# Half of a decoder's retention projection as a seven-product group, with three buffers and the first loads moved

## The chip, the cores and the metric

The kernel runs on one core of one Trainium2 chip. The metric is device time in microseconds (us), the median of several runs. A core has a matrix engine (TensorE, PE in the profile, with its weight loads as PEld), three engines for elementwise work (VectorE: DVE, ScalarE: ACT, GpSimd: POOL) and a synchronisation engine (SP) that here issues only the weight loads. All five run their own instruction streams in order and meet at semaphores. Data lies in the on-chip SBUF, matmul results in eight PSUM banks of 128 x 512 fp32.

## The reference

Two layers, each with a retention branch and an mLSTM branch that read one combined projection of x, merge gates, an output product, and a SwiGLU block; D_MODEL 1024, SEQ 512, DEPTH 2, four heads with q/k of 128 and v of 256 in each branch.

```python
for l in range(DEPTH):
    proj = x @ w_in[l]
    (r_q, r_k, r_v, r_g, m_qk, m_v, m_o, m_i, m_f, g_a, g_b) = jnp.split(proj, IN_OFFSETS, axis=-1)
    ...
    o_ret = _head_norm(_retention(rq, rk, rv), ret_norm_g[l]) * jax.nn.silu(r_g.astype(f32))
    y_ret = o_ret.astype(dt) @ w_proj_ret[l]
    ...
    y_ml = o_ml.astype(dt) @ w_proj_mlstm[l]
    gate_a = jax.nn.sigmoid(g_a + b_merge[l, :D_MODEL])
    gate_b = jax.nn.sigmoid(g_b + b_merge[l, D_MODEL:])
    mix = (gate_a * y_ret + gate_b * y_ml) @ w_out[l]
    x = _layer_norm(DEEPNORM_ALPHA * x + mix, ln1_g[l], ln1_b[l])
    gu = x @ w_gate_up[l]
    hidden = jax.nn.silu(gu[..., :D_FF]) * gu[..., D_FF:]
    x = _layer_norm(DEEPNORM_ALPHA * x + hidden @ w_down[l], ln2_g[l], ln2_b[l])
```

The change touches `y_ret` (1024 x 1024 weights times 1024 x 512 activations), and the places where other values are kept.

## The kernel before, in words

**Products in three parts.** Every fp32 number is split into a high part, rounded to the matrix engine's fp32r type, and the low rest. A product is three matmuls: high by high, high by low, low by high. The high part of a weight unit is a copy on ACT (`hi_to`, L201), the low part a subtraction on DVE (`lo_of`, L133).

**Units and groups.** Weights come in units of 128 x 1024 fp32 (512 KB), loaded by SP in a fixed order into a ring of five raw buffers; high and low parts have rings of five too, and preparation runs four units ahead. `feat` (L272) multiplies one unit with the whole activation: 24 matmuls of 512 columns into one main bank, then an evacuation. `quad` (L304) takes four units at once, as a 2 x 2 block product of the Strassen-Winograd kind: seven products p1, p3, p5, p7, p6, p2, p4, each of 24 matmuls of 256 columns, in place of eight. Its operands are four plain weight blocks and three or four sums of blocks (T1, T2, T3 on DVE in `sum_to`, L187 to L191; T4 on POOL, L223), and on the activations' side four sums of quarters, which `input_sums` makes for one block of 128 rows at a time: two additions of high and low part on POOL (`xs`, L589), four sums on DVE (`sf`, L595), a high copy on ACT and a low subtraction on DVE. Product p3 reads the fourth sum.

**Order.** PE's and SP's instructions run as the program writes them. ACT, DVE and POOL get an order from a scheduler, except inside most groups, where the written order holds. Work that PE doesn't do at once lies in a queue of generators (`side`); `slot()` runs one step of it after every few matmuls, and `drain()` what is left. The heads' attention work, the transposes, `input_sums` and `fetch` (L560 to L565: reads a branch's result back from HBM and splits it) are such generators.

**Banks.** Four PSUM banks are "main" (`pm`) and four auxiliary (`pa`). The value columns of a branch and then its gate columns are computed token by token (`tok_units`, L360 to L362) in four main banks each; head work takes auxiliary banks.

**The stage that changes.** After the merge gates, whose last groups read x, the retention result (`orh`, `orl`) is multiplied with its projection: eight `feat` calls with `ya_evac` (L912), each an evacuation on DVE that multiplies with the gate `sga`. Beside them `fetch` brings in the mLSTM result (`om`, in the big pair that is not x's), whose eight `feat` calls follow; then the mixing product reads `mx`, which lies where x was. One pool of four scratch buffers (tag `sc`) serves `xs`, `sf`, `of`, the groups' evacuations and the first x loads.

**The start.** x is loaded in six pieces, four of 128 x 512 on ACT's queue and two of 128 x 1024 on SP's, between the slices of the first four weight units (L424); ACT copies the high parts (L433), and `first_units` (L343 to L345) multiplies as the pieces land.

Of the kernel before, what the change touches and what calls it, by code (L numbers as in the profile page):

```python
# [53 lines left out]
def layer_plan():  # L54
# [34 lines left out]
    for j in range(2, FT, 2):  # L89
        for c in (0, DFF):  # L90
# [8 lines left out]
QUADS = [layer_plan().index(("F", w, c + j * P)) for w, c, js in (("in", O_MQK, (0, 2)), ("in", O_GA, (0, 4)),  # L99
                                                                  ("in", O_GB, (0, 4)), ("gu", 0, range(2, FT, 2))) for j in js]  # L100
UNIT_IF = layer_plan().index(("F", "if", 0))
# [3 lines left out]
def decoder_trunk(ctx: ExitStack, tc: tile.TileContext, wall, xT_in, x_in, pvec, lnp, rtab, out):  # L105
# [311 lines left out]
    for i in range(NFIRST):  # L417
        firsts.append([wp.tile([P, UNIT], F32, tag="raw", name="wraw", bufs=NRAW),
                       wp.tile([P, UNIT], F32R, tag="hi", name="whi"), wp.tile([P, UNIT], F32R, tag="lo", name="wlo")])
    k0 = 0  # L420
    for n in (1, 1, 1, 1, 2, 2):
        t = scratch([P, n, S], "xraw")
        ks, cs = slice(k0, k0 + n), slice(k0 * P, (k0 + n) * P)
        (nc.scalar if n == 1 else nc.sync).dma_start(t, xT_in[:, ks, :])  # L424
        for i, (r, hi, lo) in enumerate(firsts):
            nc.sync.dma_start(r[:, cs], wall[i][:, cs])
        if k0 == 0:
            nc.vector.tensor_copy(xh[:, ks, :], t)
        else:
            nc.scalar.copy(xh[:, ks, :], t)  # L430
        lo_of(xl[:, ks, :], t, xh[:, ks, :])
        for r, hi, lo in firsts:
            nc.scalar.copy(hi[:, cs], r[:, cs])  # L433
            lo_of(lo[:, cs], r[:, cs], hi[:, cs])
        k0 += n
    for i, (r, hi, lo) in enumerate(firsts):
# [22 lines left out]
    def scores(qk, hh, box, mult, key_weight, query_weight):  # L459
# [5 lines left out]
        for c in range(2):  # L465
            pa = aux_bank()
            t0, t1, t2 = c * HC, c * HC + P, (c + 1) * HC
            nc.tensor.matmul(pa[:, :HC], lhsT=k[:, t0:t1], rhs=q[:, t0:t2], start=True, stop=True)  # L468
            nc.tensor.matmul(pa[:, HC:W1], lhsT=k[:, t1:t2], rhs=q[:, t1:t2], start=True, stop=True)
            pf = scratch([P, W1], "pf")  # L470
            mult(pf, pa, c)
            hi, lo = pp[:, 2 * c * W1 : (2 * c + 1) * W1], pp[:, (2 * c + 1) * W1 : (2 * c + 2) * W1]
            nc.scalar.copy(hi, pf)
            lo_of(lo, pf, hi)
            yield
        pa = aux_bank()
        for j in range(2):
# [20 lines left out]
    def weighted(box, vh, vl, hh, nv, done):  # L498
# [3 lines left out]
        val = lambda j: (vh[:, j, hh, :], vl[:, j, hh, :])  # L502
        pa = aux_bank()
        for j in range(2):
# [5 lines left out]
        for i in range(NB):  # L510
            c, e = i // 2, i % 2
            pa = aux_bank()
            w = [(0, e * P)] + ([(1, HC)] if e else [])
            for n, (j, o) in enumerate(w):
                three(pa[:, :nv], cut(2 * c * W1 + o, P, W1), val(2 * c + j), n == 0, c == 0 and n == e)
            if c:
                three(pa[:, :nv], cut(O_QD + e * P, P, HC), st, False, True)
            done(i, pa)
            yield

    def head_norms(oo, p, gt, gain, od):
# [22 lines left out]
        for hh in range(2):  # L544
            m = 2 * (2 * p + hh)
            t = scratch([P, 2, S], "ot")
            for f in range(2):
                pa = aux_bank()
                for b in range(NB):
# [21 lines left out]
    class Halves:  # L571
# [32 lines left out]
    for l in range(L):  # L604
# [62 lines left out]
        def if_cols():  # L667
            r3 = rows[:, 3]
            pa = aux_bank()
            for b in range(NB):  # L670
# [5 lines left out]
        for p in range(2):  # L676
# [42 lines left out]

            tok_units([main_bank() for _ in range(NB)], lambda k: xh[:, k], lambda k: xl[:, k], K8, True, True, v_evac)  # L720
            oo = reg.tile([P, 2, NB, DV], F32, tag="oo", name="roo")
# [14 lines left out]

            tok_units([main_bank() for _ in range(NB)], lambda k: xh[:, k], lambda k: xl[:, k], K8, True, True, g_evac)
            drain()
            gain = pv[:, C_RG : C_RG + 8]
            side.append(head_norms(oo, p, gt, gain, od[0]))  # L740
# [42 lines left out]
        for p in range(2):  # L783
# [142 lines left out]
        mxh, mxl = bigpair(cur, f"mx{l}")

# [306 lines left out]
```

## Time and profile before

| what | value |
|---|---|
| median of three runs | 1776.27 us (1775.71 to 1776.57) |
| the profiled execution | 1776.88 us |
| its span | 1775.2 us |
| mean granted clock of PE | 0.998 |
| PE busy | 1760.3 us, 99% |
| DVE, ACT, POOL busy | 1311.3, 793.9, 432.9 us |

The page and the trace come from the profiled execution. A line of the timeline gives start and duration of an instruction in us, engine, program line, operation, output and inputs by their names, the shape, and in brackets how long the engine had been idle and what ended that. The start-to-start distance of neighbours is their cost, since durations overlap a little. A line of the waits gives who waited, for whom, total us, how often, and the longest. A line of the windows gives a stretch, the busy time of PE, PEld, DVE, ACT and POOL, the granted clock (1.00 is full) and the share and rate of the DMA engines.

### The profile page before, as it was taken

Reading aid. Unit: us, or ns where it says so; the run is one execution under the profiler, and the core shown is the slowest. Engines: PE = TensorE matmul, PEld = TensorE weight load, DVE = VectorE, ACT = ScalarE, POOL = GpSimd, SP = SyncE. Lnnn points to the kernel's source line nnn. Section 1 sums busy time; section 2 is a strip of 40 time slices with the busy share of each in tenths; the row PEclk is TensorE's granted clock in tenths of the full one; section 3 lists DMA queues with packets and bytes.
Section 4 is the critical chain, followed back from the end, with each engine's and each line's share of the span. In section 5 each row is a group of like instructions: output and inputs, shape, how many; then the busy total and the mean of one; then the engine's idle time right before and its main releaser. Section 6 shows DMA issues by size and latency. Waiting matters only on the chain.

```text
span 1775.2 us, 27167 instructions
## 1 busy us (share of the span) xinstructions
PE 1760.3 (99%) x10904; PEld 1586.0 (89%) x10904; DVE 1311.3 (74%) x1735; ACT 793.9 (45%) x1157; POOL 432.9 (24%) x321
## 2 busy tenths in 40 slices
PE   9999999999999999999999999999999999999997
PEld 7888898998889999988898898989988899999886
DVE  7686878795559999863476868787845699998534
ACT  5445555663226444451244455556533254445310
POOL 2141110231001555520121311112300115555200
PEclk9999999999999999999999999999999999999999
DMA  7222422346333333363243323313553223333521
GB/s 253 91 91 81 142 79 88 111 141 235 96 114 109 99 96 108 107 213 96 84 166 91 110 86 107 119 60 108 201 179 119 96 95 107 111 116 112 187 70 48
DMA packets 76174, 209.49 MB, mean 118 GB/s; under 512 B 6760, under 2 KB 9832, under 8 KB 75024
## 3 DMA queue, kind: packets, MB, share of 16 engines
q1 hardware_dynamic: 65632, 167.27, 29.5%
q0 software_dynamic: 9840, 39.43, 6.3%
q8 instruction: 86, 1.41, 0.3%
q10 hardware_dynamic: 576, 1.05, 0.2%
q14 instruction: 40, 0.33, 0.1%
HBM read 190.93 MB, written 16.79 MB: 117 GB/s over the span
## 4 chain that ended last, share of the span: by engine, by line
PE 97%; DVE 1%; DMA 1%; ACT 1%; issue 0%; SPq 0%; DVEq 0%
PE pm L324 31%; PE pm L360 9%; PE pm L362 9%; PE pm L361 9%; PE pm L267 5%; PE pm L266 5%; PE pm L268 5%; PE pa L324 5%; PE pa L361 3%; PE pa L360 3%; PE pa L362 3%; PE pa L494 1%; PE pa L495 1%; PE pa L496 1%; PE pa L550 1%; PE pa L468 1%
## 5 line engine op out<-in xcount | busy, mean ns | idle before, releaser
L133 DVE TENSOR_TENSOR wlo<-wraw,whi 128x1024 fp32r<-128x1024 f32 (+2 forms) x424 | 597.0, 1421 | 201.9 <-ACT whi L201 198.9
L201 ACT CAST whi<-wraw 128x1024 fp32r<-128x1024 f32 x402 | 419.9, 1049 | 471.0 <-PE pm L267 115.2
L450 POOL TENSOR_TENSOR rs<-ve,nhalf 128x4 f32<-128x4 f32 (+1 forms) x32 | 31.9, 997 | 482.6 <-DVE ve L449 482.6
L223 POOL TENSOR_TENSOR wraw<-wraw 128x1024 f32<-128x1024 f32 x32 | 77.0, 2406 | 151.2 <-issue 57.9
L360 PE MATMUL pm<-whi,x0h 128*128 128x512 f32 x256 | 102.9, 402 | 1.5 <-DVE rvl L133 1.5
L360 PE MATMUL pm<-whi,x20h 128*128 128x512 f32 x256 | 102.5, 400 | 0.6 <-DVE rvl L133 0.6
L362 PE MATMUL pm<-wlo,x0h 128*128 128x512 f32 x256 | 100.7, 393 | 0.0
L361 PE MATMUL pm<-whi,x0l 128*128 128x512 f32 x256 | 100.4, 392 | 0.0
L362 PE MATMUL pm<-wlo,x20h 128*128 128x512 f32 x256 | 100.3, 392 | 0.0
L361 PE MATMUL pm<-whi,x20l 128*128 128x512 f32 x256 | 100.1, 391 | 0.0
L1085 POOL TENSOR_TENSOR qa<-qa 128x512 f32<-128x512 f32 x20 | 42.8, 2141 | 142.6 <-DVE qa L1084 90.6
L324 PE MATMUL pm<-x10h,whi 128*128 128x256 f32 x240 | 67.9, 283 | 0.0
L324 PE MATMUL pm<-x10l,whi 128*128 128x256 f32 x240 | 67.9, 283 | 0.0
L324 PE MATMUL pm<-s0h,whi 128*128 128x256 f32 x240 | 67.9, 283 | 0.0
L324 PE MATMUL pm<-s0l,whi 128*128 128x256 f32 x240 | 67.9, 283 | 0.0
L324 PE MATMUL pm<-s0h,wlo 128*128 128x256 f32 x240 | 67.9, 283 | 0.0
L324 PE MATMUL pm<-x11h,whi 128*128 128x256 f32 x240 | 67.9, 283 | 0.0
L324 PE MATMUL pm<-x11l,whi 128*128 128x256 f32 x240 | 67.9, 283 | 0.0
L324 PE MATMUL pm<-x11h,wlo 128*128 128x256 f32 x240 | 67.9, 283 | 0.0
L324 PE MATMUL pm<-s1h,whi 128*128 128x256 f32 x240 | 67.9, 283 | 0.0
L324 PE MATMUL pm<-s1l,whi 128*128 128x256 f32 x240 | 67.9, 283 | 0.0
L324 PE MATMUL pm<-s1h,wlo 128*128 128x256 f32 x240 | 67.9, 283 | 0.0
(519 smaller groups left out, 5675.2 us busy)
## 6 DMA issues: line engine op xcount, KB each, us to landing
wraw<-wall SPq DMA_DIRECT2D x306, 512.0 KB, 3.8
od<-ot POOLq DMA_DIRECT2D x16, 512.0 KB, 3.6
of<-od POOLq DMA_DIRECT2D x16, 512.0 KB, 5.0
gb<-lnp POOLq DMA_DIRECT2D x4, 1024.0 KB, 6.2
x1d<-xr POOLq DMA_DIRECT2D x8, 512.0 KB, 2.9
xr<-x1d POOLq DMA_DIRECT2D x8, 512.0 KB, 4.8
negm<-md POOLq DMA_DIRECT2D x2, 1026.0 KB, 6.6
xr<-xtok POOLq DMA_DIRECT2D x4, 512.0 KB, 6.8
```

Source lines behind the costliest of these rows:

```text
L133: nc.vector.tensor_tensor(out=out_lo, in0=full, in1=hi.bitcast(F32), op=ALU.subtract)
L201: nc.scalar.copy(hi, sum_t[i])
L223: nc.gpsimd.tensor_tensor(out=raw_t[u + 2], in0=raw_t[u], in1=raw_t[u + 3], op=ALU.add)
L266: nc.tensor.matmul(pm[:, c0:c1], lhsT=hi[:, k], rhs=xh[:, k, c0:c1], start=(k == 0), stop=False)
L267: nc.tensor.matmul(pm[:, c0:c1], lhsT=hi[:, k], rhs=xl[:, k, c0:c1], start=False, stop=False)
L268: nc.tensor.matmul(pm[:, c0:c1], lhsT=lo[:, k], rhs=xh[:, k, c0:c1], start=False, stop=(k == KT - 1))
L324: nc.tensor.matmul(pm, lhsT=x[:, j, k], rhs=y[:, k], start=go and n == 0, stop=j == 1 and k == 3 and n == 2, skip_group_check=not first)
L360: nc.tensor.matmul(pm, lhsT=sh(k)[:, a], rhs=hi[:, j], start=first, stop=False)
L361: nc.tensor.matmul(pm, lhsT=sl(k)[:, a], rhs=hi[:, j], start=False, stop=False)
L362: nc.tensor.matmul(pm, lhsT=sh(k)[:, a], rhs=lo[:, j], start=False, stop=last)
L450: nc.gpsimd.tensor_tensor(out=rs[:, :n], in0=ve[:, :n], in1=nhalf[:, :n], op=ALU.pow)
L1085: nc.gpsimd.tensor_tensor(out=v, in0=v, in1=u, op=ALU.subtract)
```

## The change

1. The last four of the eight units of the retention projection become one seven-product group, with a new evacuation `ya_ev`: ACT copies p1 and p5, DVE takes the others, and POOL two subtractions and six multiplications with half of a gate each. It needs `input_sums` of the retention result and the sums T1 to T4 of those weights. `in_turn` interleaves these input sums with the `fetch` of the mLSTM result during the first four `feat` calls.
2. Three homes rotate: `om` takes the place of x, the new sums `rs` the place of the earlier sums, and the mixing input four tiles that held values (`vh`, `vl`), gates (`gt`) and head outputs (`oo`).
3. The gate stream (second token stream of a pair of heads) takes the four auxiliary banks, and head work during it main ones (`stream_banks`, `head_bank`).
4. All six x loads are issued on ACT's queue before anything else there; the last two go to a tile of their own, `x_late`.

Below are rows of the engines' orders, before and after. DVE around the retention stage, before: `om0l` is the low part of a fetched mLSTM piece, `sga` the evacuation of a unit.

```order
L889 TENSOR_TENSOR ga<-pm,ga 128x512
L133 TENSOR_TENSOR wlo<-wraw,whi 128x1024
L133 TENSOR_TENSOR om0l<-of,om0h 128x1024
L912 TENSOR_TENSOR sga<-pm,sga 128x512
L133 TENSOR_TENSOR om0l<-of,om0h 128x1024
L133 TENSOR_TENSOR wlo<-wraw,whi 128x1024
L912 TENSOR_TENSOR sga<-pm,sga 128x512
L133 TENSOR_TENSOR wlo<-wraw,whi 128x1024
L912 TENSOR_TENSOR sga<-pm,sga 128x512
```

And after, the last piece of the sums, up to the fourth and last `rs0l` (`sf` are the sums, the `wraw` row is T2):

```order
L608 TENSOR_TENSOR sf<-sf,xs 128x256
L144 TENSOR_TENSOR om0l<-of,om0h 128x1024
L144 TENSOR_TENSOR wlo<-wraw,whi 128x1024
L144 TENSOR_TENSOR rs0l<-sf,rs0h 128x4x256
L927 TENSOR_TENSOR sga<-pm,sga 128x512
L608 TENSOR_TENSOR sf<-xs 128x256 x2
L608 TENSOR_TENSOR sf<-sf,xs 128x256
L144 TENSOR_TENSOR wlo<-wraw,whi 128x1024
L608 TENSOR_TENSOR sf<-sf,xs 128x256
L202 TENSOR_TENSOR wraw<-wraw 128x1024
L927 TENSOR_TENSOR sga<-pm,sga 128x512
L144 TENSOR_TENSOR rs0l<-sf,rs0h 128x4x256
```

Between two evacuations stood one or two operations of 1024 columns; now there are four to seven rows, the sums among them.

POOL in the same place, after (before, it held only the fetches `of` and the loads `xr` there): the additions `xs`, two by two or four, and the weight sum T4 (`wraw`).

```order
L898 TENSOR_TENSOR ga<-ga 128x512
L899 TENSOR_TENSOR gc<-gc,ga 128x512
L602 TENSOR_TENSOR xs<-orh,orl 128x512 x2
L571 DMA of<-od 128x1024
L602 TENSOR_TENSOR xs<-orh,orl 128x512 x4
L571 DMA of<-od 128x1024
L234 TENSOR_TENSOR wraw<-wraw 128x1024
L571 DMA of<-od 128x1024
```

All additions but the first two now stand behind the last evacuation of the merge gates (`ga`, `gc`).

ACT at the start, before, with the semaphores that a row waits for:

```order
L424 DMA xraw<-xt 128x512 x3
L433 ACT_TABLE_LOAD
L433 CAST whi<-wraw 128x128 [waits DMAHW1_49]
L433 CAST whi<-wraw 128x128 [waits DMAHW2_49]
L433 CAST whi<-wraw 128x128 [waits DMAHW4_49]
L433 CAST whi<-wraw 128x128 [waits DMAHW5_49]
L430 CAST x0h<-xraw 128x512 [waits DMAHW3_49]
L433 CAST whi<-wraw 128x128 [waits DMAHW7_49]
```

And after:

```order
L434 DMA xraw<-xt 128x512 x3
L434 DMA xraw<-xt 128x512 [waits DMAHW0_49]
L434 DMA x_late<-xt 128x1024 [waits DMAHW3_49]
L434 DMA x_late<-xt 128x1024 [waits DMAHW7_49]
L445 ACT_TABLE_LOAD
L445 CAST whi<-wraw 128x128 [waits DMAHW1_49]
L445 CAST whi<-wraw 128x128 [waits DMAHW2_49]
```

The three later loads now stand ahead of the table load and of the first cast. By the casts' waits, semaphore 0 is that of the first x piece, 3 of the second, and 7 of the fifth weight slice.

The core of the diff:

```diff
-                                                                  ("in", O_GB, (0, 4)), ("gu", 0, range(2, FT, 2))) for j in js]
+                                                                  ("in", O_GB, (0, 4)), ("ret", 0, (4,)), ("gu", 0, range(2, FT, 2))) for j in js]
...
+    def head_bank():
+        return main_bank() if turned["now"] else aux_bank()
+
+    def stream_banks(second):
+        turned["now"] = second
+        return [aux_bank() if second else main_bank() for _ in range(NB)]
...
-    k0 = 0
-    for n in (1, 1, 1, 1, 2, 2):
-        t = scratch([P, n, S], "xraw")
+    x_late = reg.tile([P, 4, S], F32, tag="gt", name="x_late")
+    x_raw = [(k, 1, scratch([P, 1, S], "xraw")) for k in range(4)] + [(k, 2, x_late[:, k - 4 : k - 2]) for k in (4, 6)]
+    for k0, n, t in x_raw:
+        nc.scalar.dma_start(t, xT_in[:, k0 : k0 + n, :])
+    for k0, n, t in x_raw:
         ks, cs = slice(k0, k0 + n), slice(k0 * P, (k0 + n) * P)
-        (nc.scalar if n == 1 else nc.sync).dma_start(t, xT_in[:, ks, :])
...
-            pa = aux_bank()
+            pa = head_bank()
...
-            tok_units([main_bank() for _ in range(NB)], lambda k: xh[:, k], lambda k: xl[:, k], K8, True, True, g_evac)
+            tok_units(stream_banks(True), lambda k: xh[:, k], lambda k: xl[:, k], K8, True, True, g_evac)
             drain()
+            turned["now"] = False
...
-        omh, oml = bigpair(oth, f"om{l}")
-        side.append(fetch(od[1], [omh[:, :4], omh[:, 4:]], [oml[:, :4], oml[:, 4:]]))
-        for m in range(8):
+        def ya_ev(m):
+            t = {}
+
+            def times(src, i, half, eng):
+                for j in range(2):
+                    g = sga[m + 2 * i + j][:, half * HC : (half + 1) * HC]
+                    eng.tensor_tensor(out=g, in0=src[:, j * HC : (j + 1) * HC], in1=g, op=ALU.mult)
+
+            def ev(name, banks):
+                two = lambda n: t.setdefault(n, scratch([P, 2, S], n))
+                if name == "p1":
+                    nc.scalar.copy(two("ra")[:, 0], banks["a"])
+                elif name == "p5":
+                    nc.scalar.copy(two("ra")[:, 1], banks["c"])
+                elif name == "p7":
+                    nc.vector.tensor_tensor(out=two("rc")[:, 1], in0=t["ra"][:, 1], in1=banks["d"], op=ALU.subtract)
+                elif name == "p6":
+                    u, v = t["ra"][:, 0], t["ra"][:, 1]
+                    nc.vector.tensor_tensor(out=u, in0=banks["b"], in1=u, op=ALU.add)
+                    nc.gpsimd.tensor_tensor(out=v, in0=v, in1=u, op=ALU.subtract)
+                    nc.gpsimd.tensor_tensor(out=t["rc"][:, 1], in0=t["rc"][:, 1], in1=u, op=ALU.subtract)
+                elif name == "p2":
+                    times(banks["a"], 0, 0, nc.vector)
+                    nc.vector.tensor_tensor(out=t["rc"][:, 0], in0=banks["e"], in1=t["ra"][:, 1], op=ALU.add)
+                elif name == "p4":
+                    nc.vector.tensor_tensor(out=t["ra"][:, 1], in0=banks["d"], in1=t["ra"][:, 0], op=ALU.add)
+
+                    def rest():
+                        times(t["rc"][:, 0], 1, 0, nc.gpsimd)
+                        times(t["rc"][:, 1], 1, 1, nc.gpsimd)
+                        times(t["ra"][:, 1], 0, 1, nc.gpsimd)
+                    return rest
+            return ev
+
+
+        omh, oml = bigpair(cur, f"om{l}")
+        rsh, rsl = sum_views(oth, f"rs{l}")
+        pending = [input_sums(Halves(orh), Halves(orl), rsh, rsl), fetch(od[1], [omh[:, :4], omh[:, 4:]], [oml[:, :4], oml[:, 4:]])]
+
+        def in_turn():
+
+            n = 0
+            while pending:
+                n += 1
+                for g in pending[:1] * (n % 2) + pending[-1:] if len(pending) > 1 else list(pending):
+                    if next(g, "end") == "end":
+                        pending.remove(g)
+                yield
+
+        side.append(in_turn())
+        for m in range(4):
             feat(Halves(orh), Halves(orl), ya_evac(m))
+        with tc.manual_schedule(engines=ordered):
+            quad(Halves(orh), Halves(orl), rsh, rsl, ya_ev(4))
         drain()
...
-        mxh, mxl = bigpair(cur, f"mx{l}")
+        mxs = [reg.tile([P, 4, S], F32R, tag=t, name=f"mx_{t}") for t in ("vh", "vl", "gt", "oo")]
+        mxh, mxl = Halves(mxs[:2]), Halves(mxs[2:])
```

More of the change, by code (lines that the diff above doesn't have):

```diff
@@ L122, in aux_bank @@
         return psa.tile([P, 512], F32, tag="a", name="pa")
+    turned = {"now": False}
+    def head_bank():
[3 more added lines that the diff above has]
+        return [aux_bank() if second else main_bank() for _ in range(NB)]
     def scratch(shape, name):
@@ L434, in decoder_trunk @@
             lo_of(lo[:, cs], r[:, cs], hi[:, cs])
-        k0 += n
     for i, (r, hi, lo) in enumerate(firsts):
@@ L475, in scores @@
             yield
-        pa = aux_bank()
+        pa = head_bank()
         for j in range(2):
@@ L502, in weighted @@
         val = lambda j: (vh[:, j, hh, :], vl[:, j, hh, :])
-        pa = aux_bank()
+        pa = head_bank()
         for j in range(2):
@@ L511, in weighted @@
             c, e = i // 2, i % 2
-            pa = aux_bank()
+            pa = head_bank()
             w = [(0, e * P)] + ([(1, HC)] if e else [])
@@ L547, in head_norms @@
             for f in range(2):
-                pa = aux_bank()
+                pa = head_bank()
                 for b in range(NB):
@@ L577, in __getitem__ @@
         def __getitem__(self, a):
+            if isinstance(a[1], slice):
+                return self.ts[a[1].start // 4][:, :, a[2]]
             return self.ts[a[1] // 4][:, a[1] % 4, a[2]] if len(a) == 3 else self.ts[a[1] // 4][:, a[1] % 4]
@@ L668, in if_cols @@
             r3 = rows[:, 3]
-            pa = aux_bank()
+            pa = head_bank()
             for b in range(NB):
@@ L718, in v_evac @@
                 lo_of(vl[:, b], src, vh[:, b])
-            tok_units([main_bank() for _ in range(NB)], lambda k: xh[:, k], lambda k: xl[:, k], K8, True, True, v_evac)
+            tok_units(stream_banks(False), lambda k: xh[:, k], lambda k: xl[:, k], K8, True, True, v_evac)
             oo = reg.tile([P, 2, NB, DV], F32, tag="oo", name="roo")
@@ L827, in v_evac @@
                 lo_of(vl[:, b, :, :DV], src, vh[:, b, :, :DV])
-            tok_units([main_bank() for _ in range(NB)], lambda k: xh[:, k], lambda k: xl[:, k], K8, True, True, v_evac)
+            tok_units(stream_banks(False), lambda k: xh[:, k], lambda k: xl[:, k], K8, True, True, v_evac)
             oo = reg.tile([P, 2, NB, DV], F32, tag="oo", name="moo")
@@ L850, in g_evac @@
                 nc.scalar.activation(gt[:, b], pm, AF.Sigmoid)
-            tok_units([main_bank() for _ in range(NB)], lambda k: xh[:, k], lambda k: xl[:, k], K8, True, True, g_evac)
+            tok_units(stream_banks(True), lambda k: xh[:, k], lambda k: xl[:, k], K8, True, True, g_evac)
             drain()
+            turned["now"] = False
             gain = pv[:, C_MG : C_MG + 8]
```

## The prediction, made before the result was known

> **What bounds the kernel now.** I read the page first, then the chain of waits, then PE's own waits, and last the timeline of the stage that is changed.
>
> ```profile
> span 1775.2 us, 27167 instructions
> PE 1760.3 (99%) x10904; PEld 1586.0 (89%) x10904; DVE 1311.3 (74%) x1735; ACT 793.9 (45%) x1157; POOL 432.9 (24%) x321
> PE 97%; DVE 1%; DMA 1%; ACT 1%; issue 0%; SPq 0%; DVEq 0%
> PE pm L360 <- DVE rvl L133: 2.0, 2, 1.5
> PE pm L344 <- DVE wlo L133: 1.6, 2, 0.8
> ```
>
> PE is busy for 99% of the span and is 97% of the chain; its waits are a few us in all. So the end moves by what is taken from PE's matmuls and by any wait that is newly put in front of them. DVE's 74% is a mean; what counts is DVE's load in the 22 us in which the new sums have to be made.
>
> The sum below is made against the profiled execution (1776.88 us, of which the span is 1775.2), 0.6 above the median of 1776.27. A measurement of this kernel can tell about 0.2%, 3.6 us, from no change.
>
> **1. Fewer matmuls in the retention projection.** Eight units run today from the first `orh` matmul to the first `om0h` one:
>
> ```profile
> 404.93 0.40 PE L266 MATMUL pm<-orh,whi 128*128 128x512 f32 x1
> 449.46 0.40 PE L266 MATMUL pm<-om0h,whi 128*128 128x512 f32 x1
> 359.01 17.28 PE pm L324 x144
> 376.29 2.88 PE pa L324 x24
> ```
>
> That is 44.53 us for 192 matmuls, or 0.232 each; four units take 22.27. The chain of waits shows a group of seven products without a gap: 144 matmuls in 17.28 and 24 in 2.88, so 168 in 20.16. Saved: 2.11 per layer, **-4.2** in two layers. If no wait arose, this would be all of it.
>
> **2. The sums of the retention activations, made on DVE and POOL.** The second product (p3) takes the fourth sum, in four blocks of 128 rows. Its first three blocks occupy 9 matmuls of 0.12 us, so PE needs the last block's lo part at 404.93 + 22.27 + 2.88 + 1.08 = 431.2. Is it there? DVE works in its own order. From the end of the evacuation at 404.09 (L887 before, L902 now) to the fourth `rs0l`, the change puts in DVE's queue: 14 operations of 1024 columns (5 `wlo`, 3 weight sums T1 to T3, 2 `om0l`, 4 `rs0l`), 5 evacuations of 512 with a PSUM source, and 16 `sf` of 256. Prices, start to start:
>
> ```profile
> 101.81 0.41 DVE L595 TENSOR_TENSOR sf<-sf,xs 128x256 f32<-128x256 f32 x1
> 102.14 1.21 DVE L133 TENSOR_TENSOR wlo<-wraw,whi 128x1024 fp32r<-128x1024 f32 x1
> 103.28 0.41 DVE L595 TENSOR_TENSOR sf<-sf,xs 128x256 f32<-128x256 f32 x1
> 404.09 0.69 DVE L887 TENSOR_TENSOR gc<-pm,ga 128x512 f32<-128x512 f32 x1 [1.19 <-POOL ga L883]
> 404.70 1.69 DVE L133 TENSOR_TENSOR om0l<-of,om0h 128x1024 fp32r<-128x1024 f32 x1
> 404.50:448.60 44.10, 44.10 (x194) 35.83 (x194) 21.58 (x22) 15.22 (x20) 4.03 (x7) 1.00 0.58 198
> ```
>
> 0.33 for a `sf` (101.81 to 102.14), 1.14 for 1024 columns (102.14 to 103.28), 0.61 for a PSUM evacuation (404.09 to 404.70). So 16.0 + 3.0 + 5.3 = 24.3 us of DVE work from 404.7 on: it ends at 429.0, 2.2 us ahead of PE, if DVE is never held. The windows view (PE, PEld, DVE, ACT, POOL, the clock) says that today DVE is busy 21.58 of the whole 44.1 us there; the change wants more than that in the first half.
>
> DVE is held, by POOL. The change puts 8 additions `xs` of 512 columns (two of them while DVE still works for the group before) and the weight sum T4 on POOL:
>
> ```profile
> 401.86 2.20 POOL L883 TENSOR_TENSOR ga<-ga 128x512 f32<-128x512 f32 x1 [1.00 <-DVE ga L882]
> 404.02 1.29 POOL L884 TENSOR_TENSOR gc<-gc,ga 128x512 f32<-128x512 f32 x1
> 616.89 1.22 DVE L133 TENSOR_TENSOR wlo<-wraw,whi 128x1024 fp32r<-128x1024 f32 x1
> 625.98 7.57 DVE L133 TENSOR_TENSOR wlo<-wraw,whi 128x1024 fp32r<-128x1024 f32 x3
> 625.59 2.41 POOL L223 TENSOR_TENSOR wraw<-wraw 128x1024 f32<-128x1024 f32 x1 [2.35 <-issue]
> 627.96 4.52 POOL L1067 TENSOR_TENSOR hf_vl<-qb,qc 128x512 f32<-128x512 f32 x2
> ```
>
> Three `wlo` that should take 3 x 1.14 = 3.4 took 7.57 beside 2.41 + 4.52 us of POOL, while POOL's own additions stretched from 1.29 (at 404.02, beside an evacuation that took its usual 0.69) to 2.26 each. Two operations that both read SBUF run in turn, not together; one with a PSUM source isn't touched. So I add POOL's time to DVE's: 8 x 1.29 + 2.4 = 12.7, less at most 3.0 that falls beside the five evacuations: 9.7 to 12.7. DVE ends at 438.7 to 441.7, PE waits 7.5 to 10.5. Bounds: 0 (no sharing cost) and 10.5. I take **9.0 per layer, +18.0**, nearest to the row of 7.57. A wait can't be under nothing. What is queued behind on DVE (the weights' lo parts of later products, 1.14 each against 2.88 per product) catches up. The four casts on ACT and the three more hi copies lie beside this: ACT is busy 15.22 of 44.1 there. The six half-width multiplications of the new evacuation are on POOL behind the group's last product, and nobody waits for them before the mixing stage.
>
> The Trainium skill ("GPSIMD Engine Reference", section 1, Specifications) says that GpSimd's SBUF interfaces are shared with VectorE, with contention against instructions that have two SBUF inputs. The trace agrees, with 7.57 for 3.4 and an untouched 0.69 with a PSUM input. By that rule the sum stays as it is.
>
> **3. The clock after a wait.** One stall today shows what a pause costs beyond itself:
>
> ```profile
> 59.68 0.50 PE L360 MATMUL pm<-whi,x0h 128*128 128x512 f32 x1 [1.47 <-DVE rvl L133]
> 60.26:63.67 3.41, 3.41 (x13) 2.93 (x12) 2.51 (x4) 0.42 (x2) 0.00 (x0) 0.50 0.57 163
> 63.67:67.08 3.41, 3.41 (x20) 2.93 (x19) 1.03 (x3) 0.54 (x2) 0.00 (x0) 1.00 0.32 129
> 940.54 0.50 PE L360 MATMUL pm<-whi,x20h 128*128 128x512 f32 x1 [0.57 <-DVE rvl L133]
> ```
>
> After 1.47 us of idleness PE ran 3.41 us at a granted clock of 0.50, which loses half of it, 1.7. A wait of 9 us should bring that at least once: **+1.7 per layer, +3.4**, bounds 0 and 6.8 (two windows each).
>
> The Trainium skill ("TensorE: Matmul & The Clock Gate", Part 1) puts the drop behind at least one idle window of about 3.4 us. Here it followed on 1.47 us, so the measurement decides. By the page, waits of 9 us drop the clock too.
>
> **4. The second stream's banks.** The gate stream no longer waits for the values' evacuation: it starts in the auxiliary banks, and the head work takes main ones. The 1.47 of layer 0, its 1.7 of half clock and the 0.57 of layer 1 are on offer, 3.7. But six matmuls later (1.4 us) the first head product stands in a main bank and reads `rvl` blocks that come from DVE in the same row of evacuations, 0.6 apart; I leave 0.8 in. **-2.9**, bounds 0 and -3.7.
>
> **5. The start.** All six x loads stand at the head of ACT's queue. The fourth to sixth wait, by the order, for the first x, the second x and the fifth weight slice to land, and the table load and the first cast are queued behind:
>
> ```profile
> 0.81 1.37 ACTq L424 DMA_DIRECT2D xraw<-xt  x3
> ...
> 2.21 1.28 ACT L433 ACT_TABLE_LOAD   x1 [2.21 <-issue]
> 4.17 0.30 ACT L433 CAST whi<-wraw 128x128 fp32r<-128x128 f32 x1 [0.69 <-DMA wraw<-wall]
> 5.00 0.77 PE L343 MATMUL pm<-x0h,whi 128*128 128x512 f32 x1
> 6.61 0.67 ACT L433 CAST whi<-wraw 128x128 fp32r<-128x128 f32 x2 [1.31 <-DMA wraw<-wall]
> 7.71 0.69 ACT L433 CAST whi<-wraw 128x128 fp32r<-128x128 f32 x3
> 18.55 0.50 PE L344 MATMUL pm<-x0h,wlo 128*128 128x512 f32 x1 [0.80 <-DVE wlo L133]
> 30.71 0.39 PE L285 MATMUL pm<-x0h,whi 128*128 128x512 f32 x1
> ```
>
> The third slice had landed at 6.61 and the fifth (first of the three at 7.71) by 7.71; I take 7.2. Add one DMA issue (1.37 / 3 = 0.5), the table load 1.28 and the 0.83 from first cast to first matmul (4.17 to 5.00): PE begins at 9.8 instead of 5.00, +4.8 (4.2 to 5.3). Against it: the first four units ran from 5.00 to 30.71, 25.7 us for 96 matmuls that at 0.232 take 22.3. Up to 3.4 us of waits, such as that at 18.55, go if x is early and the later start lets the weights get ahead. And PE, whose warming matmuls end before the first cast is there, may begin at half clock (+1.7, as in part 3). Bounds +1.4 (4.8 - 3.4) and +6.5 (4.8 + 1.7); I take **+2.5**.
>
> **6. Homes.** The rotated buffers add no operation. `om` now goes where x was, and x is read until 404.93, so its copies begin some 4 us later; PE wants them after the retention stage, 20 us and more behind that. `rs` takes the place of the earlier sums, and the mixing input that of values, gates and head outputs, done by then. Priced at 0, hidden by the four feats and the group; without that cover it is one wait of about an `om0l`, 1.7.
>
> Sum: -4.2 + 18.0 + 3.4 - 2.9 + 2.5 = +16.8, so 1776.9 + 16.8 = **1793.7**.
>
> **Rivals.**
> *A, DVE gets there (faster).* Place: p3's fourth block; price: no wait. It decides if POOL's 12.7 cost DVE less than 2.2 us. For it: DVE alone ends at 429.0, and two `xs` come early. Against it: the 7.57 row. -4.2 - 2.9 + 2.5 = -4.6: 1772.3.
> *B, a partial wait.* POOL's additions fall into DVE's gaps; 4 us per layer and no clock drop: -4.2 + 8 - 2.9 + 2.5 = +3.4: 1780.3. Against it: DVE's queue has hardly a gap before 429.
> *C, full waits, clock kept.* +16.8 - 3.4: 1790.3. For it: the 0.57 at 940.54 left the clock alone. Against: 1.47 did not.
> *D, worse.* POOL and DVE pass four scratch buffers to and fro (`xs`, `sf`, the fetched `of` and the evacuation's own), so each also waits for the other: 12 per layer, the start at +6.5 and nothing from the banks: -4.2 + 24 + 3.4 + 6.5 = +29.7: 1806.6.
> That the change doesn't do what it says I leave out: PE's order holds 144 rows more, 2 x (168 - 96).
>
> **How the numbers follow.** Forecast 0.55, A 0.15, B 0.10, C 0.12, D 0.08. The forecast's own range, with PE's waits of 7.5 to 10.5 and the bounds of the start, is 1786 to 1802. For 8 in 10 I leave out A and half of D: 1776 to 1805. Faster by over 0.2% means below 1772.7: most of A, 0.13. Within 0.2%: the rest of A and most of B, 0.09. Slower: 0.78.
>
> **What would show it.** Right: PE waits in the second product of both retention groups for `rs0l` from DVE, 7 to 11 us each, with a clock of 0.50 behind them; three lo operations or sums stretched beside `xs`; the first matmul at 9 to 10; no wait of the gate stream for `rvl`. Wrong: a retention group that runs in 20.2 us without a wait (A), or a wait that ends on ACT or a DMA instead of DVE.

## The result and the profile after

The changed kernel takes 1794.07 us (median of four runs, 1793.69 to 1794.6) against 1776.25 for the kernel before: a ratio of 1.0103, 95% interval 1.0090 to 1.0115. It is slower by 17.8 us, and its profiled span is 1792.4 us against 1775.2, 17.2 more.

The head of the page:

```profile
span 1792.4 us, 27563 instructions
PE 1761.0 (98%) x11048; PEld 1596.0 (89%) x11048; DVE 1365.2 (76%) x1791; ACT 810.4 (45%) x1175; POOL 494.9 (28%) x355
```

PE's waits (who waited, for whom, total us, how often, longest):

```profile
PE pm L335 <- DVE rs0l L144: 4.4, 2, 3.1
PE pm L354 <- ACT whi L445: 4.3, 1, 4.3
PE pm L335 <- DVE rs1l L144: 4.2, 2, 3.0
PE pm L335 <- ACT rs0h L609: 3.7, 1, 3.7
PE pm L335 <- ACT rs1h L609: 3.6, 1, 3.6
```

PE's busy time has hardly moved although it has fewer columns to stream, which already says that part of it runs more slowly. The wait for `rvl` is gone from the list. New are 8.0 us (layer 0: 4.4 + 3.7) and 7.8 us (layer 1) at L335, the group's matmuls, and 4.3 at the first matmul. PE's timeline at those places, layer 0:

```profile
9.13 0.80 PE L354 MATMUL pm<-x0h,whi 128*128 128x512 f32 x1 [4.34 <-ACT whi L445]
...
404.80 0.40 PE L277 MATMUL pm<-orh,whi 128*128 128x512 f32 x1
...
427.01 0.28 PE L335 MATMUL pm<-orh,whi 128*128 128x256 f32 x1
...
432.19 0.38 PE L335 MATMUL pm<-rs0l,whi 128*128 128x256 f32 x1 [1.31 <-DVE rs0l L144]
...
436.35 0.58 PE L335 MATMUL pm<-rs0h,whi 128*128 128x256 f32 x1 [3.65 <-ACT rs0h L609]
439.98 0.58 PE L335 MATMUL pm<-rs0l,whi 128*128 128x256 f32 x1 [3.05 <-DVE rs0l L144]
...
458.23 0.39 PE L277 MATMUL pm<-om0h,whi 128*128 128x512 f32 x1
```

The retention stage lasts from 404.80 to 458.23, 53.43 us, where it was 44.53. By the rates of before its matmuls need 22.27 + 20.16 = 42.43; 8.0 are the three waits, inside p3: for the low part of the third block of the sums, and for the high and then the low part of the fourth; 3.0 are left. The windows view shows most of what those are (columns as before; the clock is the third number from the end):

```profile
435.00:438.00 3.00, 0.58 (x1) 0.29 (x1) 3.00 (x4) 2.60 (x5) 1.50 (x1) 0.50 0.26 25
438.00:441.00 3.00, 1.02 (x5) 1.02 (x6) 3.00 (x3) 0.94 (x1) 1.35 (x2) 0.50 0.65 217
441.00:444.00 3.00, 3.00 (x16) 3.00 (x16) 2.33 (x3) 0.79 (x1) 0.53 (x1) 0.50 0.66 184
444.00:447.00 3.00, 3.00 (x23) 3.00 (x23) 2.36 (x2) 1.24 (x3) 0.06 (x1) 0.86 1.01 388
```

The clock is at 0.50 from 435 until after 444. And this is why the sums were late, on DVE and POOL:

```profile
410.27 2.29 DVE L198 TENSOR_TENSOR wraw<-wraw 128x1024 f32<-128x1024 f32 x1
...
419.94 1.22 DVE L144 TENSOR_TENSOR wlo<-wraw,whi 128x1024 fp32r<-128x1024 f32 x1
...
421.42 0.68 DVE L927 TENSOR_TENSOR sga<-pm,sga 128x512 f32<-128x512 f32 x1
423.95 0.76 DVE L608 TENSOR_TENSOR sf<-xs 128x256 f32<-128x256 f32 x2 [1.85 <-POOL xs L602]
...
426.43 2.33 DVE L144 TENSOR_TENSOR om0l<-of,om0h 128x1024 fp32r<-128x1024 f32 x1
428.68 2.32 DVE L144 TENSOR_TENSOR wlo<-wraw,whi 128x1024 fp32r<-128x1024 f32 x1
430.93 1.21 DVE L144 TENSOR_TENSOR rs0l<-sf,rs0h 128x1024 fp32r<-128x1024 f32 x1
...
436.87 3.05 DVE L144 TENSOR_TENSOR rs0l<-sf,rs0h 128x1024 fp32r<-128x1024 f32 x1
```

POOL's timeline of the same stretch:

```profile
410.18 3.54 POOL L602 TENSOR_TENSOR xs<-orh,orl 128x512 f32<-128x512 f32 x2 [2.76 <-ACT sgb L884]
...
419.11 4.80 POOL L602 TENSOR_TENSOR xs<-orh,orl 128x512 f32<-128x512 f32 x2 [0.36 <-DVE rs0l L144]
426.26 3.66 POOL L602 TENSOR_TENSOR xs<-orh,orl 128x512 f32<-128x512 f32 x2 [2.35 <-DVE rs0l L144]
...
436.50 2.34 POOL L234 TENSOR_TENSOR wraw<-wraw 128x1024 f32<-128x1024 f32 x1 [6.08 <-ACT rs0h L609]
```

Beside the `xs` at 410 and 426 and beside T4, DVE's operations of 1024 columns take 2.29 to 3.05 instead of 1.2. Beside the `xs` at 419 it is the other way round: DVE's `wlo` at 419.94 takes its usual 1.22, the two `xs` take 4.80, and DVE is then idle for 1.85 us until they are done. From 406.80 to the end of the last `rs0l` at 439.92 that is DVE's only pause. And the last two pairs of `xs` wait for an `rs0l` on DVE, which frees their scratch buffer: so the two engines hold each other up in that way too. The cast on ACT for which PE waits 3.65 us is itself late because of DVE: it starts as soon as DVE's last `sf` is done.

```profile
435.25 1.04 ACT L609 CAST rs0h<-sf 128x1024 fp32r<-128x1024 f32 x1 [0.23 <-DVE sf L608]
```

Where the time went, stage by stage, from the starts of PE's matmuls in the two traces:

| stage | before | after | difference |
|---|---|---|---|
| to the end of the first units | 30.71 | 33.66 | +2.95 |
| from there to the sums of the first mLSTM group (173.06, 172.94) | 142.35 | 139.28 | -3.07 |
| retention stage, layer 0 | 44.53 | 53.43 | +8.90 |
| mixing product, layer 0 | 45.32 | 45.78 | +0.46 |
| its end to the next layer's first matmul | 349.34 | 348.98 | -0.36 |
| layer 1, to the sums of its first mLSTM group | 164.71 | 164.06 | -0.65 |
| retention stage, layer 1 | 44.53 | 53.24 | +8.71 |
| mixing product, layer 1 | 45.32 | 45.77 | +0.45 |
| all others | | | -0.2 |

### The profile page after: what moved, and what is told of

Read it like the earlier page. It is cut to its first block, busy times and chain, and to the rows that moved or that the text cites. A ratio compares the mean times of both kernels' runs of the same rounds, so it can differ in the third digit from the quotient of the medians.

```text
span 1792.4 us, 27563 instructions
## 1 busy us (share of the span) xinstructions
PE 1761.0 (98%) x11048; PEld 1596.0 (89%) x11048; DVE 1365.2 (76%) x1791; ACT 810.4 (45%) x1175; POOL 494.9 (28%) x355
## 5 line engine op out<-in xcount | busy, mean ns | idle before, releaser
L144 DVE TENSOR_TENSOR wlo<-wraw,whi 128x1024 fp32r<-128x1024 f32 (+2 forms) x430 | 613.2, 1440 | 211.2 <-ACT whi L212 205.8
L212 ACT CAST whi<-wraw 128x1024 fp32r<-128x1024 f32 x408 | 426.7, 1049 | 453.2 <-PE pa L372 104.6
L234 POOL TENSOR_TENSOR wraw<-wraw 128x1024 f32<-128x1024 f32 x34 | 81.6, 2400 | 163.7 <-issue 57.9
L335 PE MATMUL pm<-x10h,whi 128*128 128x256 f32 x240 | 67.9, 283 | 0.0
L335 PE MATMUL pm<-x10l,whi 128*128 128x256 f32 x240 | 67.9, 283 | 0.0
L335 PE MATMUL pm<-s0h,whi 128*128 128x256 f32 x240 | 67.9, 283 | 0.0
L335 PE MATMUL pm<-s0l,whi 128*128 128x256 f32 x240 | 67.9, 283 | 0.0
L335 PE MATMUL pm<-s0h,wlo 128*128 128x256 f32 x240 | 67.9, 283 | 0.0
L335 PE MATMUL pm<-x11h,whi 128*128 128x256 f32 x240 | 67.9, 283 | 0.0
L335 PE MATMUL pm<-x11l,whi 128*128 128x256 f32 x240 | 67.9, 283 | 0.0
L335 PE MATMUL pm<-s1h,whi 128*128 128x256 f32 x240 | 67.9, 283 | 0.0
L335 PE MATMUL pm<-s1l,whi 128*128 128x256 f32 x240 | 67.9, 283 | 0.0
L335 PE MATMUL pm<-s1h,wlo 128*128 128x256 f32 x240 | 67.9, 283 | 0.0
L335 PE MATMUL pm<-x10h,wlo 128*128 128x256 f32 x240 | 67.9, 283 | 0.0
L335 PE MATMUL pm<-x11h,wlo 128*128 128x256 f32 x240 | 67.9, 283 | 0.0
L202 DVE TENSOR_TENSOR wraw<-wraw 128x1024 f32<-128x1024 f32 x34 | 52.3, 1538 | 0.0
L371 PE MATMUL pa<-whi,x0h 128*128 128x512 f32 x128 | 51.4, 402 | 0.0
L371 PE MATMUL pa<-whi,x20h 128*128 128x512 f32 x128 | 51.4, 402 | 0.0
L634 POOL TENSOR_TENSOR rqk<-rqk,rt 128x512 f32<-128x512 f32 x16 | 33.3, 2082 | 65.1 <-DVE rt L633 65.1
L371 PE MATMUL pm<-whi,x0h 128*128 128x512 f32 x128 | 51.1, 399 | 0.0
```

Source lines behind the costliest of these rows:

```text
L144: nc.vector.tensor_tensor(out=out_lo, in0=full, in1=hi.bitcast(F32), op=ALU.subtract)
L202: nc.vector.tensor_tensor(out=f, in0=f, in1=e, op=ALU.add)
L212: nc.scalar.copy(hi, sum_t[i])
L234: nc.gpsimd.tensor_tensor(out=raw_t[u + 2], in0=raw_t[u], in1=raw_t[u + 3], op=ALU.add)
L335: nc.tensor.matmul(pm, lhsT=x[:, j, k], rhs=y[:, k], start=go and n == 0, stop=j == 1 and k == 3 and n == 2, skip_group_check=not first)
L371: nc.tensor.matmul(pm, lhsT=sh(k)[:, a], rhs=hi[:, j], start=first, stop=False)
```

## The experiments

Times are medians, each beside the median of the kernel before on the same chip.

| kernel | us | before | difference |
|---|---|---|---|
| the change | 1794.07 | 1776.25 | +17.8 |
| x loads put back | 1793.56 | 1775.35 | +18.2 |
| group taken out | 1776.12 | 1775.35 | +0.8 |
| `xs` on DVE | 1787.14 | 1775.35 | +11.8 |
| `xs` as a copy on ACT | 1772.90 | 1775.35 | -2.5 |
| banks alone | 1772.99 | 1776.33 | -3.3 |
| start alone | 1776.42 | 1776.33 | +0.1 |
| idle matmuls in p3 | 1792.06 | 1776.33 | +15.7 |
| group in the mLSTM projection | 1772.52 | 1776.33 | -3.8 |
| x loads put back, `x_late` kept | 1791.88 | 1776.02 | +15.9 |
| mLSTM group, `x_late` kept | 1770.14 | 1776.02 | -5.9 |
| mLSTM group, start as changed | 1773.40 | 1776.07 | -2.7 |
| mLSTM group, late x on POOL's queue | 1770.42 | 1776.07 | -5.7 |

**Is it the group?** The change with eight plain units:

```diff
-("ret", 0, (4,)), ("gu", ...
+("gu", ...
...
-        for m in range(4):
+        for m in range(8):
             feat(Halves(orh), Halves(orl), ya_evac(m))
-        with tc.manual_schedule(engines=ordered):
-            quad(Halves(orh), Halves(orl), rsh, rsl, ya_ev(4))
```

> The change without the seven-product group: eight plain units in the retention projection, no input sums; homes, banks and start as changed. Theory (the whole loss is the group's waits on DVE and the clock behind them): 1776.3 - 3.7 (banks) + 3.0 (start) = 1775.5 us, 1774.5 to 1777, no PE wait in the retention stage. Rival (the rotated homes, by the later fetch of the mLSTM result and the mixing input in four tiles, carry a part of the loss, as the 0.4 us more in each mixing stage hints): over 1777.5 us, with PE waits on om or mx.

1776.12, ratio 1.0002 (0.9992 to 1.0011), and PE waits for nothing behind the first units. So 17 of the 17.8 us come with the group. The fetch into the rotated homes makes no wait; the 0.5 us in each mixing stage stays (below).

**Is it POOL and DVE keeping each other out?** Two runs that take `xs` from POOL. First to DVE:

```diff
-                nc.gpsimd.tensor_tensor(out=t[:, i], ...
+                (nc.vector if which == "rs" else nc.gpsimd).tensor_tensor(out=t[:, i], ...
```

> The change with the eight additions xs of each retention stage on DVE instead of POOL; same result, same buffers. Theory (an addition of two SBUF inputs on POOL keeps DVE out for its whole 1.29 us, while on DVE it costs 0.6): although DVE gets 8 x 0.6 = 4.9 us more to do, its last low part comes earlier, since 8 x 1.29 = 10.3 us of exclusion go; PE waits 4 to 6.5 us per layer instead of 8.0, time 1786 to 1791 us. Rival (POOL's additions run beside DVE and only DVE's own load counts): DVE ends 4 to 5 us later, waits of 12 to 13 us, time 1802 to 1804 us.

1787.14, ratio 1.0063 (1.0048 to 1.0078): more work on the busiest helper, and 6.0 us gained on the change. DVE's low part of the last block and T4, and PE's waits in layer 0:

```profile
432.75 0.70 DVE L927 TENSOR_TENSOR sga<-pm,sga 128x512 f32<-128x512 f32 x1
433.36 3.01 DVE L144 TENSOR_TENSOR rs0l<-sf,rs0h 128x1024 fp32r<-128x1024 f32 x1
```

```profile
432.94 2.35 POOL L234 TENSOR_TENSOR wraw<-wraw 128x1024 f32<-128x1024 f32 x1 [8.40 <-DVE wlo L144]
```

```profile
433.07 0.38 PE L335 MATMUL pm<-rs0h,whi 128*128 128x256 f32 x1 [2.10 <-ACT rs0h L609]
436.42 0.58 PE L335 MATMUL pm<-rs0l,whi 128*128 128x256 f32 x1 [2.97 <-DVE rs0l L144]
```

5.1 us of waits instead of 8.0. Of them T4 alone holds the last `rs0l` for 1.8 (3.01 against 1.2). Then to ACT, as a copy of the high part:

```diff
+                if which == "rs":
+                    nc.scalar.copy(t[:, i], xh[:, m + 4 * i].bitcast(F32))
```

> The change with the additions xs replaced by copies of the high part on ACT (the low part of the retention result is left out of the sums, so four output blocks are a little less exact); buffers and order of the sums otherwise as they are. Theory (sharing between POOL and DVE): DVE alone needs 24.3 us plus at most the 2.4 of T4, so PE waits 0 to 3 us per layer instead of 8.0; time 1777 to 1784 us. Rival (the four scratch buffers handed to and fro between xs, sf and of decide, whoever makes xs): waits of 6 us or more stay, time over 1789 us.

1772.90, ratio 0.9986 (0.9977 to 0.9995): faster than the expected 1777 to 1784. The sums of this run leave out the low part of the retention result, so it shows a cause and is not the same computation.

```profile
404.09 1.71 DVE L144 TENSOR_TENSOR wlo<-wraw,whi 128x1024 fp32r<-128x1024 f32 x1
...
428.37 3.12 DVE L144 TENSOR_TENSOR rs0l<-sf,rs0h 128x1024 fp32r<-128x1024 f32 x1
```

```profile
431.55 0.39 PE L335 MATMUL pm<-rs0l,whi 128*128 128x256 f32 x1 [0.95 <-DVE rs0l L144]
```

DVE's queue from 404.09 to the end of the fourth low part now takes 27.4 us: the forecast's 24.3 of its own, 1.9 for T4 beside the last `rs0l`, and the rest a wait of 0.6 for a load and the 0.5 by which the first `wlo` is stretched. PE waits 0.95, and the clock stays. Buffers and their order are the same as in the change. So POOL's `xs` are the cause of most of the waits, and the number of scratch buffers is not. The two runs by themselves don't part the collision of POOL and DVE from POOL's being slow, since an `xs` on ACT takes only 0.6 us. The rows of the change do: of the 8.8 us by which DVE's queue there exceeds 24.3, about 4.4 are DVE operations stretched beside `xs`, 1.8 the one beside T4, 0.5 the first `wlo` beside a gate addition, and 1.85 idleness in which DVE waits for an `xs`. Whether a fifth buffer would save a part of these wasn't tried.

**Is the rest half clock?** Extra matmuls of no use, ahead of the second, third and fourth block of p3:

```diff
+                    if warm and name == "p3" and j == 0 and k:
+                        if k == 1:
+                            pw = aux_bank()
+                        for _ in range((warm // 3, warm, warm)[k - 1]):
+                            nc.tensor.matmul(pw[:, :256], lhsT=hi[:, 0, 0], rhs=ah[:, 0], start=True, stop=True)
```

> The change with extra matmuls of no use on PE inside p3 of each retention group: 8, 24 and 24 of 256 columns into a spare bank ahead of its second, third and fourth block, to fill the pauses of 1.3, 3.7 and 3.1 us. Theory (the pause itself is set by DVE, and what the stage loses beyond the 8.0 us of waits is half clock): the same DVE chain, so the group's blocks start when they did, but the matmuls behind them run at full clock: 1.5 to 3 us less per layer, 1788 to 1791 us, although PE does 6.7 us more work per layer. Rival (the rest of the loss isn't the clock): 1793.5 us or more.

1792.06, ratio 1.0091 (1.0074 to 1.0108): 2.1 us less than the change by the two differences, where 3 to 6 were expected. They fill the first two pauses. The last one, inside the fourth block, they only shorten, since none stands between its high and its low part. Here it is in layer 0 and in layer 1:

```profile
440.72 0.39 PE L340 MATMUL pm<-rs0l,whi 128*128 128x256 f32 x1 [2.19 <-DVE rs0l L144]
...
1327.60 0.39 PE L340 MATMUL pm<-rs1l,whi 128*128 128x256 f32 x1 [1.91 <-DVE rs1l L144]
```

Layer 1 of the two traces, the change first:

```profile
1322.00:1326.00 4.00, 0.58 (x1) 0.29 (x1) 4.00 (x5) 3.58 (x5) 2.05 (x1) 0.51 0.25 52
1326.00:1330.00 4.00, 2.57 (x12) 2.57 (x13) 4.00 (x4) 0.39 (x1) 1.35 (x3) 0.50 0.65 210
```

```profile
1322.00:1326.00 4.00, 3.69 (x31) 3.48 (x29) 4.00 (x5) 3.68 (x5) 1.92 (x1) 1.00 0.18 47
1326.00:1330.00 4.00, 2.40 (x20) 2.40 (x21) 4.00 (x4) 1.00 (x2) 1.51 (x3) 1.00 0.64 213
```

There the clock stayed at 1.00, and the stage took 51.20 us instead of 53.24: 2.0 gained by 6.7 us of useless work. In layer 0 the clock fell behind the pause of 2.19 all the same (0.62 of full speed from 441 to 444); that stage took 52.95, 0.5 less.

The starts in the change's own trace say the same. A matmul of the group takes 0.12 us (20.16 / 168), and 34 stand ahead of the one that starts at 439.98; from 427.01 on they would have brought PE there at 431.09. So the last operand is 8.9 us late, of which the three waits are 8.0 (layer 1: 8.7 and 7.8). The 134 matmuls from there to 458.23 take 18.25 us instead of 16.08, in both layers: 2.2 us of half clock. So of the 3.0 us, 2.2 are half clock behind the last wait, and the other 0.8 or 0.9 lie between the waits, at the edges of the pauses.

**Banks and start, each alone.** On the kernel before:

> The kernel before with one part of the change: the gate streams take the auxiliary banks, head work takes main ones meanwhile. Theory (the stalls of 1.47 and 0.57 us and 3.4 us of half clock were waits for a main bank): 3.1 us less before the mLSTM sums of layer 0 and 0.65 less in layer 1, so 3.7 us less than the kernel before on the same chip, 3 to 4. Rival (the gain comes back at the next wait, as the small difference of the change without its group, 0.8 us over the kernel before, leaves open): less than 1.5 us.

1772.99, ratio 0.9982 (0.9973 to 0.9992), 3.3 us less, and no wait for `rvl`.

> The kernel before with one part of the change: all six x loads first on ACT's queue. Theory (first matmul at 9.1 instead of 5.0, half clock behind the pause, some later waits gone): 2.9 us more than the kernel before on the same chip, 2 to 4. Rival (the loss is made up behind the first units, since putting the loads back into the change gained only 0.5 us against the two kernels' own before): within 1 us.

1776.42, ratio 1.0006 (0.9996 to 1.0015). The rival was right, but not for a general reason. The trace:

```profile
9.30 0.79 PE L343 MATMUL pm<-x0h,whi 128*128 128x512 f32 x1 [4.39 <-ACT whi L434]
...
61.09 0.50 PE L360 MATMUL pm<-whi,x0h 128*128 128x512 f32 x1 [0.38 <-DVE rvl L133]
```

The start does lose time (the first units end at 33.20 instead of 30.71), but the stall on the values' banks shrinks from 1.47 to 0.38, and no half clock follows it: by the first mLSTM sums the loss is gone (172.94 against 173.06). With the banks turned there is no such stall to shrink. That was tried in the kernel that is described last, with its group in the mLSTM projection; this run has the x loads as the change has them, its sibling has them on the queues and in the order of before:

> The group in the mLSTM projection, with the x loads as the change has them (all six first on ACT's queue). No stall on the values' banks is left that a late start could shorten. Theory (the late start costs its 2.5 to 2.9 us wherever no later wait takes it up): first matmul at about 9, 5.9 - 2.9 = 3 us under the kernel before on the same chip, 2.5 to 4. Rival (a late start is made up in any case): 5.5 us under it or more.

1773.40, ratio 0.9982 (0.9972 to 0.9991): 2.7 us under before, where its sibling with early casts is 5.9 under. So there the late start costs 3.2 (2.7 by the spans of the two profiles).

**Putting the x loads back, and places in SBUF.**

```diff
-    for k0, n, t in x_raw:
-        nc.scalar.dma_start(t, xT_in[:, k0 : k0 + n, :])
+        (nc.scalar if n == 1 else nc.sync).dma_start(t, xT_in[:, ks, :])
```

> The change with only the x loads put back as they were (four pieces on ACT's queue between its casts, two on SP's). Theory (ACT's table load and first cast stand behind three loads that wait; the first feats lose 2.95 us of stage time, 30.71 against 33.66): 1794.1 - 2.9 = 1791.1 us, within 1790 to 1792, first matmul at about 5.0. Rival (the weights' arrival sets the end of the first units, so that the late start is made up anyway or shows elsewhere): no difference, 1793.5 to 1794.6.

1793.56, 18.2 over its before (1.0100, 1.0083 to 1.0117): a miss. The retention stage of layer 0 began 2.8 us earlier (401.97 against 404.80), and the end came no earlier. The trace shows the loss in stages where PE never waits: 46.5 us in each mixing stage against 45.8, 0.35 to 0.5 in the groups. (Of the retention stages, one took 0.9 us less than in the change and the other 0.9 more.) Without `x_late`, tiles are allocated otherwise, so they presumably stand elsewhere in SBUF; the traces have no addresses. One and the same group of matmuls, `mx_vh` into a main bank, in the change, in this run and in the next, by duration of one:

```profile
L371 PE MATMUL pm<-whi,mx_vh 128*128 128x512 f32 x32 | 12.8, 400 | 0.0
```

```profile
L371 PE MATMUL pm<-whi,mx_vh 128*128 128x512 f32 x32 | 13.0, 405 | 0.0
```

```profile
L371 PE MATMUL pm<-whi,mx_vh 128*128 128x512 f32 x32 | 12.8, 400 | 0.0
```

In the kernel before, with `mx` in one big pair, it is 394. The next run loads x as this one, but into `x_late`:

> The change with the x loads in the old order and on the old queues, as in the run with the start put back, but with the last two pieces in the tile x_late, as in the change. So the tiles of values, gates, head outputs and scratch stand at the changed kernel's places in SBUF, which they did not in that run. Theory (the start costs 2.9 us, and that run lost its gain again because its tiles stood elsewhere: its mixing stages took 46.5 us instead of 45.8, its groups of gates and of the feed-forward block about 0.35 to 0.5 more): first matmul at 5.0, mixing stages at 45.8, 1790 to 1791.5 us against 1794.1. Rival (the loss behind an early start has to do with when things run, not where they lie): mixing stages at 46.5 again, 1793 us or more.

1791.88, ratio 1.0088 (1.0075 to 1.0102). The mixing stages are at 45.78 and 45.77, as the theory of places has it, and the time is 0.4 us over its range. In the profiled execution of this run, PE met a wait of 1.74 us at 20.88, in the first units, and half clock behind it, so that the first units ended at 34.22; in the run before, with the same loads, they ended at 29.97. The four times lie between 1789.4 and 1794.1, and the profiled one is the slowest. So the old start is no sure gain here. That the four times differ by such a wait is not shown, since only one was profiled.

**A better place for the group.** The retention projection plain, the last four units of the mLSTM projection as a group:

```diff
-("ret", 0, (4,)), ("gu", ...
+("ml", 0, (4,)), ("gu", ...
...
+        side.append(fetch(od[1], [omh[:, :4], omh[:, 4:]], [oml[:, :4], oml[:, 4:]]))
+        side.append(input_sums(omh, oml, rsh, rsl))
+        for m in range(8):
+            feat(Halves(orh), Halves(orl), ya_evac(m))
...
+        for m in range(4):
+            feat(omh, oml, mix_evac(m))
+        drain()
+        with tc.manual_schedule(engines=ordered):
+            quad(omh, oml, rsh, rsl, yb_ev(4))
```

> Another place for the group: the retention projection as eight plain units, and the last four units of the mLSTM projection, which runs behind it, as the seven-product group, whose input sums (of the mLSTM result) follow its fetch and have the 44 us of the retention stage and four feats behind it; x loads as before, banks and homes as changed; its last multiplications on DVE. Theory (the change lost for want of DVE and POOL time in 22 us): no PE wait on the sums, the group's 2.1 us per layer come in: the kernel before less 4.2 less 3.7 (banks) plus 0.9 (homes) = 7 us less, 5 to 8. Rival (the group's own preparation, weight sums and evacuation, costs what it saves wherever it stands): no gain beyond the banks', 3 us or less.

1772.52, ratio 0.9981 (0.9972 to 0.9990). No wait on the sums, as the theory had it, but 3.8 us gained instead of 5 to 8. Two sizes were off. The mLSTM stage went from 43.57 to 41.96: plain units there take 0.227 per matmul, not 0.232, so a group saves 1.6 and not 2.1. And this kernel loads x without `x_late`, with mixing stages of 46.5. With `x_late` put in:

> The group in the mLSTM projection, as in the run before with x loads as in the kernel before, and now with the last two x pieces in x_late, so that the tiles stand at the other places. Theory (places in SBUF): 0.7 us less in each mixing stage and 0.35 less in each feed-forward block than that run, so 2.1 us more of gain: 5.5 to 6.5 us under the kernel before on the same chip. Rival: places don't matter, 3.8 us under it as before, 3.3 to 4.3.

1770.14, ratio 0.9965 (0.9951 to 0.9979): 5.9 us less than the kernel before and 24 less than the change. The mixing stages fell from 46.5 to 45.8. Of the 5.9, 3.3 are what the banks bring alone. The last run puts the three late x loads on POOL's queue:

> As the run before, but the last three x loads on POOL's queue instead of ACT's, so that ACT's table load and first casts have no waiting load ahead of them, and x is still asked for early. Theory (what delays the start is the place in ACT's queue): first matmul at 5 to 6, and x lands early enough that fewer waits follow; 5 to 7.5 us under the kernel before. Rival (the first weight slices are starved by x's early loads, from whichever queue): first matmul at 7 or later, 4 us under it or less.

1770.42, ratio 0.9967 (0.9954 to 0.9979), no different. Its first matmul is at 5.00, so it is the place on ACT's queue that delays the start; then PE waits 1.94 us at 11.41 for a cast of weights, which makes up what early x brings.

## Why the prediction was right

The forecast was 1793.7 with the profile's own base; 1794.07 was measured. As a difference, +16.8 was forecast and +17.8 measured (17.2 by the spans): the base was 0.6 above the median, and that the absolute times meet within 0.4 is partly luck. The forecast's own range of 1786 to 1802 is wider than the bounds it names for the waits and the start, which give 1789.6 to 1800.7; the result lies in both. Term by term:

| term | forecast | measured | from |
|---|---|---|---|
| fewer matmuls, per layer | -2.1 | -2.0 | `xs` on ACT: stage of 43.51 less its wait of 0.95, against 44.53 |
| waits on the sums, per layer | +9.0 (7.5 to 10.5) | last operand late by 8.9, 8.7; PE's waits 8.0, 7.8 | starts; PE's waits |
| half clock, per layer | +1.7 | 2.2; 2.0 | starts; idle matmuls in p3 |
| banks | -2.9 | -3.1 and -0.65 | stages; alone -3.3 |
| start | +2.5 | +2.95 | stage |
| homes | 0 | +0.46, +0.45, less 0.36 | stages |

*Part 2* carries the result, and its ledger held. DVE's fourth low part was forecast to end at 438.7 to 441.7; it ended at 439.92 (436.87 + 3.05), and with POOL's additions taken away DVE's own load came to the forecast 24.3 us plus T4. POOL was to cost DVE 9.7 to 12.7 us. It cost 2.1 ahead of the stage, where the two early `xs` stand, and 8.8 within it, 10.9 together. These are the rows ahead of the stage, in the kernel before and in the change:

```profile
394.70 3.60 DVE L133 TENSOR_TENSOR wlo<-wraw,whi 128x1024 fp32r<-128x1024 f32 x3
...
394.69 5.71 DVE L144 TENSOR_TENSOR wlo<-wraw,whi 128x1024 fp32r<-128x1024 f32 x3
394.72 4.60 POOL L602 TENSOR_TENSOR xs<-orh,orl 128x512 f32<-128x512 f32 x2 [1.80 <-DVE orl L144]
```

But it held in part by other ways. 1.85 of the 8.8 is idleness, in which DVE waits for two `xs` that took 4.80 and could begin only behind an `rs0l`; that the two engines wait for each other, the forecast left to rival D. And the middle one of the three waits ends on ACT's cast of `rs0h`. The forecast hadn't named that, and a wait that ends on ACT was one of its signs of being wrong; the sums ahead of the cast on DVE were what came late, so the mechanism stands. *Rival A* needed POOL to cost DVE under 2.2 us; from 406.80 to 439.92 are 33.1 us, so it cost about 7 beyond the 24.3, and 1.85 of idleness. *Rival B*'s gaps don't exist: DVE is full but for the 1.85, and those are a wait for POOL. *Rival C* is out, the clock fell in both layers.

*Part 3*: the forecast's 1.7 was a little low; 2.2 us per stage are half clock behind the last wait.

*Part 5* mis-sized the interplay, though not the sum. The terms of start and banks were added as if each stood alone. Alone, the start costs 0.1, because the stall of part 4 takes its loss up. In the change the banks remove that stall, and both the loss of 2.95 and the gain of 3.07 show in the stages. Together they are worth no more in layer 0 than the start alone: the sums of the first mLSTM group begin at 172.94 in both, against 173.06 before and 170.05 with the banks alone. Had the banks not been part of it, +2.5 would have been wrong by all of it.

*Part 6* put the homes at nothing, with a wait as the price. There was no wait; the mixing matmuls themselves became slower by 1%.

## What to carry to other kernels

A cheaper matmul scheme is worth what its preparation costs on the other engines in the window in front of it: add up the operations that stand in that engine's own order, from the stage's begin to the last operand, and add POOL's time to DVE's wherever both read two operands from SBUF. If that comes out longer than PE's work in front, move the group to a stage with more time ahead (here one projection later, which with the old x loads in `x_late` turned +17.8 us into -5.9, 3.3 of them the banks'), or take the work off POOL: even on DVE, the busier of the two, it cost 6 us less. And two parts of a change that touch the same stall are not to be added: measure one with the other in and out.

## What was not expected of the hardware

- The same matmuls, never waiting, take 394, 400 or 405 ns in kernels that allocate their tiles differently; the mixing stages of 192 matmuls take 45.3, 45.8 and 46.5 us. The allocation is shown to decide: the home of two x pieces alone moved it from 46.5 to 45.8, with the order and the queues of the loads unchanged, in two pairs of kernels. That it is the place in SBUF, and why, isn't shown.
- More work on the fullest helper made the kernel faster by 6 us (`xs` from POOL to DVE), and 6.7 us of useless matmuls in a pause made a stage faster by 2.0, by keeping the clock.
- A pause of 1.47 us halved the clock for 3.4 us in the kernel before, a pause of 1.91 us in layer 1 of the run with idle matmuls did not. By the Trainium skill ("TensorE: Matmul & The Clock Gate", Part 1) the windows that decide it run free of the program; these runs agree that the length of a pause alone doesn't decide, but here the drop followed on a pause far shorter than the idle window of about 3.4 us that the Trainium skill names there.
